# Which engine computes the exact rest of every weight group: VectorE for all of them, where GpSimd had most

## The chip, the cores and the metric

The kernel runs on one core of one Trainium2 chip. The metric is the device time of one execution in microseconds (us). Each core has TensorE (PE in the profile; its weight loads are PEld), VectorE (DVE), ScalarE (ACT), GpSimd (POOL) and SyncE (SP, which here only issues loads). An engine works through its own instructions in the order in which they were issued and waits on semaphores for the others.

## The reference: what is computed

One layer of a decoder with two groups of heads, for a prompt of 512 tokens with 16 meta tokens ahead of it, and for 8 decode sequences of one new token with 2048 cached positions each. Everything is float32.

```
z = rmsnorm(h, norm_g) @ w_in                    # (528 + 8 tokens, 2048) @ (2048, 8192)
hq, hf, hi, hg, aq, ak, av, ag = split(z)        # 8 heads of 128 columns each
o_hg = hgrn2(hq, hf, hi, state)                  # recurrent state 128x128 per head
p  = softmax(q k / 8 + bias[distance])           # two softmaxes per head: keys of 64, values of 128
o_at = (p[0] - lam * p[1]) @ v                   # prompt: 528 keys; decode: 2048 cached keys in pages + 1
h  = h + concat(norm(o_hg) * silu(hg), norm(o_at) * silu(ag)) @ w_out
y  = rmsnorm(h, final_norm_g)
```

The new keys and values, the recurrent states and `y` are the outputs. A page holds 128 cached positions of one sequence (512 KB of keys, 512 KB of values); 8 sequences have 16 pages each, so 128 key pages and 128 value pages are read.

## The kernel before, in words

**The dense product.** The columns of `w_in` make 64 blocks of 128 output features (in the order aq0-7, ak0-7, av0-7, then hf, hi, hq per head, then hg0-7, ag0-7), those of `w_out` 16 more. A block has four *groups* of four contraction chunks. TensorE reaches float32 accuracy in three products of the short type float32r: inputs and weights are each cut into a rounded part and the exact rest (xh and xl, hi and lo), and `group` issues hi·xh, hi·xl and lo·xh, 24 products in all. `split(u)` makes the two parts of group u's weights: ScalarE copies the raw weights into `hi`, rounding them, and then `lo = raw - hi` is one TENSOR_TENSOR of 128x512 on VectorE or GpSimd. Line 291 to 292, `lo_on_dve`, says on which. Both parts have four buffers; the split runs LEAD = 3 groups ahead of the product, so the write of `lo` for group u+3 waits until the product of group u-1 has been read.

**The order of issue.** The loop over u (line 1172) issues in each *slot*: `split(u + 3)`, `group(u)`, one stage of every chain that can go on (`step_threads`: prompt attention, HGRN, norms, the softmax of a decode sequence), and then `fill()`. At the end each engine is tied to the order in which its instructions were issued (line 1223).

**Decode attention on VectorE.** A key page is one multiplication of 128x1024 with the broadcast query (`pgt<-pgt,qb`) and one reduction (`scd<-pgt`). A value page is eight instructions of 128x128, one per head: `acc += page * weight` (SCALAR_TENSOR_TENSOR; for a sequence's first page TENSOR_SCALAR). `steps` lists the 256 passes: the keys run three sequences ahead of the values, and the last 48 passes are the values of sequences 5, 6 and 7. `page_step` issues half a pass. After a sequence's values `pv_end` sums `acc` over the partitions with eight products `t_o`; the next sequence's values reuse the one `acc` buffer and so wait for them.

**The planner.** `fill()` issues page passes while `clock["dve"] < clock["pe"] + LATE`. `Clock` and `Counted` keep rough costs for every instruction issued, per engine; they decide only the order. An instruction counted on VectorE takes the place of page passes in that slot.

**The loop at the end of the input blocks.** In the last slots of `w_in` (block 63 = ag7, from its second group on, line 1181) everything that the gated outputs need must have been issued: a `while` loop calls `step_threads()` and `page_step()` until the norms of both halves are in (`hnorm`, `dnorm`). Only then come groups 1 to 3 of block 63, the split of the gated outputs (mh, ml) and the 16 blocks of `w_out`. Any page passes still left at that point are issued inside this loop, between two groups of TensorE.

Of the kernel before, what the change touches and what calls it, by code (L numbers as in the profile page):

```python
# [20 lines left out]
KC = D // P            # contraction chunks  # L21
SEQ = 512
NS = 8                 # decode sequences
NM = 16                # meta tokens
# columns: meta tokens, prompt, decode; the blocks whose meta tokens reach no output leave those out
CK = NM + SEQ + NS
CQ = SEQ + NS
S0 = SEQ               # first decode column without meta columns
K0 = NM + SEQ          # and with them
# [8 lines left out]
W = 656                # period of the bias row: a strip's 528 columns and 127 rows  # L38
# [9 lines left out]
def shape_constants():  # L48
    """Matrices that depend on the shapes alone."""
    ident = np.eye(P, dtype=np.float32)  # L50
    t = np.arange(P)
    pair = ((t[:, None] // CHUNK == t[None, :] // CHUNK) & (t[:, None] <= t[None, :])).astype(np.float32)
    scan = np.ones((P, CK), np.float32)
    scan[:, 0] = 0.0
    scan[:, NM:K0:CHUNK] = 0.0
    scan[:, K0:] = 0.0
    cst = np.concatenate([ident, pair, scan], axis=1)
    # one-hot rows of buckets (row 32: masked) for: the prompt's bias row, decode's far, near and new keys
    x = np.arange(W)
    dist = 400 - np.where(x < 528, x, x - W)  # L60
    strip = np.where(dist >= 0, rel_bucket(dist), 32)
    far = np.full(P, rel_bucket(np.array(129)))
    near = rel_bucket(P - np.arange(P))
    new = np.zeros(P, np.int64)
    cols = np.concatenate([strip, far, near, new])
    oh = (np.arange(33)[:, None] == cols[None, :]).astype(np.float32)
    return cst, oh
# [6 lines left out]
class Clock:  # L74
    """Rough times at which the engines finish what has been issued, for the order of issue."""
# [11 lines left out]
    def tile(self, t, tag, bufs):  # L87
        """A tile in a ring of buffers: its first writer waits for the readers of the buffer's last tile."""
        ring = self.rings.setdefault(tag, [])
        name = t.tensor.name  # L90
        if len(ring) == bufs:
            old = ring.pop(0)
            self.read[name] = max(self.read.get(old, (0.0, ""))[0], self.written.get(old, (0.0, ""))[0]), ""
        ring.append(name)
        return t
# [15 lines left out]
    def arrive(self, ap, mb):  # L111
        """A load that is issued now."""
        start = max(self.now["dma"], self.now["pe"], self.now["dve"])
        self.now["dma"] = start + mb * 3.0
        self.written[ap.tensor.name] = self.now["dma"] + 2.0, "dma"


class Counted:
    """An engine whose instructions' rough times are kept."""
# [33 lines left out]
def layer_kernel(ctx: ExitStack, tc: tile.TileContext, A):  # L153
# [20 lines left out]
    def expln():  # L174
        """The table with both the exponential and the logarithm."""
        if table[0] != EXPLN:
            nc.scalar.preload_act_table_set(EXPLN)
            table[0] = EXPLN
            clock.now["act"] += 1.3
# [49 lines left out]
    def keep_warm(n):  # L229
        """Products that nobody reads, for TensorE's clock."""  # L230
        for _ in range(n):
            T.matmul(warm[:, :P], ones, ones, start=True, stop=True)

# [1 line left out]
    GK = 4  # L235
    NPB = 6                     # pages on chip
    NG = KC // GK
    LEAD = 3                    # groups by which the split of the weights runs ahead
# [5 lines left out]
    blocks = []                 # (name, weights, halves of columns)  # L244
# [17 lines left out]
    LASTP = ((0, 256), (256, CQ))       # the last block in parts, so that little is left to store at the end  # L262
# [5 lines left out]
    def load_raw(i):  # L268
        """Half of a block's weights."""
        b, z = divmod(i, 2)  # L270
        if b < NB:
            raws[i] = wp.tile([P, KC // 2, P], F32, name="raw", tag="raw", bufs=3)
            clock.arrive(raws[i], 0.5)
            (store if i > 2 else load)(out=raws[i], in_=blocks[b][1][z * D // 2:(z + 1) * D // 2, :].rearrange("(k p) n -> p k n", p=P))

    def split(u):
        """High part of a group of weights, rounded to float32r, and the exact rest."""
# [13 lines left out]
    def lo_on_dve(b, g):  # L291
        return b == 1 or (0 < b < 8 and g % 2 == 0) or (b >= NIN and g == 1)
# [55 lines left out]
    # the norm's weights to every partition; to columns for the meta and decode tokens  # L348
# [34 lines left out]
    # the first block's first half runs while the rest of the prompt is transposed  # L383
# [46 lines left out]
    # the small parameters  # L430
# [19 lines left out]
    dp = hw.tile([P, 2, 64], F32, name="dp", tag="dp")  # L450
    dlv = dl.rearrange("p (a b c) -> p a b c", a=2, b=2)
    nlam = cp.tile([P, 1], F32, name="nlam")      # minus lambda
# [12 lines left out]
    def small_constants():  # L465
# [15 lines left out]
        # the prompt's bias by distance, negated: a row per head, skewed through DRAM into a strip per head  # L481
# [31 lines left out]
    aq = mp.tile([P, H, CQ], F32, name="aq")            # -q/8, then the attention half of mixed  # L513
    ak = [None] * H
    hgm = [None] * H                                      # the HGRN half of mixed
# [9 lines left out]
    ktail = [cp.tile([P, 2 * NM], F32, name=f"kt{i}") for i in range(2)]     # the last keys of a head, its two parts apart  # L525
# [4 lines left out]
    # Each group of the dense product is followed by one stage of every chain that can go on; decode  # L530
    # attention's passes over pages fill VectorE up to the time that TensorE has reached.
# [27 lines left out]
    def fill():  # L559
        """Passes over pages until VectorE's work reaches to TensorE's present time."""  # L560
# [8 lines left out]
    def later(slots, **k):  # L569
        """A store some slots from now, so that its queue's engine needn't wait."""  # L570
        def gen():
            yield slots
            store(**k)
        spawn(gen())

# [7 lines left out]
    KA = 3                      # sequences by which the keys run ahead of the values  # L583
# [29 lines left out]
    def page_step():  # L613
        """Half of a page's pass."""
# [115 lines left out]
    def to_tok(src, h, name, tag, dst, dst_s):  # L730
        """Rows 0..511 in four blocks, the last 16 and decode's in a fifth."""
# [18 lines left out]
    def norm_chain(o, n, g, name, sq=None):  # L750
        """o *= g / sqrt(mean over partitions of o^2 + eps)"""
# [33 lines left out]
    def attn():  # L785
        live = {}
        for n in range(4 * H + 4):
# [6 lines left out]
            if i4:                      # output of the block  # L794
# [10 lines left out]
            if i3:                      # transposed weights  # L805
# [11 lines left out]
            if i1:                      # exponentials  # L817
# [4 lines left out]
            if n < 4 * H:               # scores  # L822
# [12 lines left out]
            if i2:                      # difference of the two softmaxes  # L835
# [10 lines left out]
            if n < 4 * H:               # maximum  # L846
# [193 lines left out]
    def mix_split(k, c0, c1):  # L1040
        """Columns of the gated outputs in two exact parts, in place of the inputs'."""
# [8 lines left out]
    def decode_norm(k0):  # L1050
        """The decode columns of a half of mixed, gated."""
# [8 lines left out]
    def decode_mix(gg):  # L1060
        """The decode columns of four heads of mixed, in two exact parts."""
# [12 lines left out]
    def out_load(q):  # L1074
        """A quarter of the residual's columns."""
# [11 lines left out]
    def squares(q, j0, j1, s):  # L1087
        """Sums of squares; ScalarE and VectorE take turns."""
        for j in range(j0, j1):
            square(xr[q][:, j, :], P, stat[0][:, j, q:q + 1], j % 2)  # L1090
        if s:
            square(xsm[q], NS, stat[0][:NS, 4, q:q + 1], True)
# [33 lines left out]
    def out_last(z, ps):  # L1126
        """A half of the last block and the norm of its tokens."""
# [129 lines left out]
```

## Time and profile before

| | |
|---|---|
| runs (us) | 1349.47, 1352.16, 1352.70: median 1352.16 |
| the profiled execution, first to last instruction | 1346.6 us |
| TensorE busy, share of the span | 1218.8 us, 91% |
| weight loads | 1150.8 us, 85% |
| VectorE busy | 946.8 us, 70% |
| GpSimd busy | 590.0 us, 44% |
| ScalarE busy | 545.0 us, 40% |
| mean granted TensorE clock | 0.951 |

The runs lie 2.9 to 6.1 us above the profiled span; the median lies 5.6 us above it. A share of the span is an average over stages: the start, key pages beside the attention projections, prompt attention, HGRN, the gate blocks, and the output projection.

### The profile page before, as it was taken

The numbers are of one execution on the slowest core, as the hardware profiler recorded it, in microseconds if no ns is written. First come the engines' busy times: TensorE is split into PE (matmuls) and PEld (weight loads), VectorE is DVE, ScalarE is ACT, GpSimd is POOL, SyncE is SP. The second block draws the span as 40 slices with busy tenths as digits, with TensorE's granted clock in tenths as the row PEclk, the third lists the DMA queues.
The fourth block names the chain that finished last, engine by engine and source line by source line (L and its number), as shares of the span: only waits on it lengthen the run. The fifth ranks groups of instructions, "written<-read, shape, count | busy, mean of one in ns | idle before, by whom it ended". The sixth has DMA issues, their size and how long they took to land. (4 is left out here: it accounts for less than half of the span.)

```text
span 1346.6 us, 25420 instructions
## 1 busy us (share of the span) xinstructions
PE 1218.8 (91%) x9260; PEld 1150.8 (85%) x9260; DVE 946.8 (70%) x1945; ACT 545.0 (40%) x1286; POOL 590.0 (44%) x415
## 2 busy tenths in 40 slices
PE   8999999999999999889979897989973849999995
PEld 6999999887787999789979897889973849999995
DVE  7410899977787879989999999999996544222123
ACT  6322232365566635445535443434310115232233
POOL 3123455422222434345343442534789684344350
PEclk9999999999999999899998998979986969999998
DMA  6453899844544567677786768769676532732323
GB/s 214 121 137 99 304 351 308 281 154 143 150 144 141 187 190 236 217 247 227 233 261 223 241 211 259 237 208 297 205 244 202 179 111 87 232 92 79 95 79 128
DMA packets 240961, 261.05 MB, mean 194 GB/s; under 512 B 8783, under 2 KB 198962, under 8 KB 240171
## 3 DMA queue, kind: packets, MB, share of 16 engines
q1 hardware_dynamic: 57298, 164.09, 36.3%
q10 hardware_dynamic: 183538, 95.34, 25.0%
q8 instruction: 73, 1.20, 0.4%
q14 instruction: 52, 0.43, 0.1%
HBM read 245.94 MB, written 16.14 MB: 195 GB/s over the span
## 5 line engine op out<-in xcount | busy, mean ns | idle before, releaser
L128 POOL TENSOR_TENSOR lo<-raw,hi 128x512 fp32r<-128x512 f32 x288 | 477.3, 1663 | 693.3 <-ACT hi L128 546.6
L128 PE MATMUL ps<-xh,hi 128*128 128x264 f32 (+2 forms) x2048 | 555.3, 300 | 9.1 <-ACT hv L128 5.7
L128 PE MATMUL ps<-xl,hi 128*128 128x264 f32 (+2 forms) x2048 | 535.6, 290 | 1.1 <-DVE xl L128 1.1
L128 PEld LDWEIGHTS ps<-xh,hi 128*128 128x128 f32 x2048 | 398.5, 195 | 26.3 <-issue 9.9
L128 PEld LDWEIGHTS ps<-xl,hi 128*128 128x128 f32 x2048 | 398.6, 195 | 5.2 <-issue 3.8
L128 PE MATMUL ps<-xh,lo 128*128 128x264 f32 (+2 forms) x2048 | 341.6, 290 | 43.5 <-POOL lo L128 43.5
L128 DVE SCALAR_TENSOR_TENSOR acc<-pgt,wd,acc 128x128 f32<-128x128 f32 x960 | 365.9, 452 | 0.0
L128 PEld LDWEIGHTS ps<-xh,lo 128*128 128x128 f32 x2048 | 292.8, 194 | 43.9 <-POOL lo L128 43.9
L128 ACT CAST hi<-raw 128x512 fp32r<-128x512 f32 x321 | 195.4, 616 | 291.2 <-PE ps L128 180.3
L128 DVE TENSOR_TENSOR pgt<-pgt,qb 128x1024 f32<-128x1024 f32 x128 | 172.4, 1347 | 38.4 <-DMA pgt<-in_cache_k 29.8
L128 DVE TENSOR_REDUCE scd<-pgt 128x16 f32<-128x1024 f32 x128 | 155.4, 1214 | 2.3
L128 PE MATMUL ps<-mh,hi 128*128 128x256 f32 (+1 forms) x512 | 130.0, 286 | 3.0 <-ACT gate L128 1.5
L128 PE MATMUL ps<-ml,hi 128*128 128x256 f32 (+1 forms) x512 | 128.5, 283 | 0.0
L128 PEld LDWEIGHTS ps<-mh,hi 128*128 128x128 f32 x512 | 96.4, 188 | 3.9 <-ACT gate L128 1.7
L128 PEld LDWEIGHTS ps<-ml,hi 128*128 128x128 f32 x512 | 96.5, 188 | 0.0
L128 DVE TENSOR_TENSOR lo<-raw,hi 128x512 fp32r<-128x512 f32 x33 | 34.8, 1059 | 79.7 <-ACT hi L128 79.3
L128 DVE TENSOR_TENSOR xr<-xr,t_y 128x512 f32<-128x512 f32 (+1 forms) x17 | 11.2, 656 | 112.3 <-PE t_y L128 112.3
L128 PE MATMUL ps<-mh,lo 128*128 128x256 f32 (+1 forms) x512 | 82.4, 283 | 0.0
L128 PEld LDWEIGHTS ps<-mh,lo 128*128 128x128 f32 x512 | 70.3, 188 | 0.0
L128 DVE SCALAR_TENSOR_TENSOR p<-p,r,p 128x144 f32<-128x144 f32 (+3 forms) x32 | 18.1, 566 | 41.6 <-ACT p L128 41.5
L128 ACT COPY hgm<-ho 128x128 f32<-128x128 f32 x32 | 8.5, 265 | 86.0 <-PE ho L128 86.0
L128 DVE TENSOR_SCALAR acc<-pgt,wd 128x128 f32<-128x128 f32 x64 | 21.4, 402 | 29.2 <-PE t_o L128 29.2
(227 smaller groups left out, 1214.0 us busy)
## 6 DMA issues: line engine op xcount, KB each, us to landing
pgt<-in_cache_k SPq DMA_DIRECT2D x128, 512.0 KB
pgt<-in_cache_v SPq DMA_DIRECT2D x128, 512.0 KB
raw<-in_w_in ACTq DMA_DIRECT2D x125, 512.0 KB
raw<-in_w_out ACTq DMA_DIRECT2D x32, 512.0 KB
x<-in_x_prompt SPq DMA_DIRECT2D x4, 1024.0 KB
qb<-qd SPq DMA_DIRECT2D x8, 512.0 KB
sd<-in_state_hgrn SPq DMA_DIRECT2D x8, 512.0 KB
vb<-hvd SPq DMA_DIRECT2D x8, 512.0 KB
```

The source lines that it names most:

```text
L128: r = f(*a, **k)
```

## The change

`lo_on_dve` returns True for every group. Before, VectorE had block 1, the even groups of blocks 2 to 7 and one group in four of `w_out`; GpSimd had the rest. Comments and docstrings are taken out as well. No number of the planner is touched, but it now counts every `lo` on VectorE.

```
     def lo_on_dve(b, g):
-        return b == 1 or (0 < b < 8 and g % 2 == 0) or (b >= NIN and g == 1)
+        return True
```

In the listings below, `lo` is a rest, `pgt` a page, `scd` the scores of a sequence, `acc` the sum over value pages; `x8` is eight instructions of the same form.

On VectorE, at the first key pages (beside the blocks of the new keys). Before:

```order
L128 TENSOR_TENSOR pgt<-pgt,qb 128x1024
L128 TENSOR_REDUCE scd<-pgt 128x16
L128 TENSOR_TENSOR pgt<-pgt,qb 128x1024
L128 TENSOR_REDUCE scd<-pgt 128x16
L128 TENSOR_TENSOR pgt<-pgt,qb 128x1024
```

The same place in the change:

```order
L128 TENSOR_REDUCE scd<-pgt 128x16
L128 TENSOR_TENSOR pgt<-pgt,qb 128x1024
L128 TENSOR_TENSOR lo<-raw,hi 128x512
L128 TENSOR_REDUCE scd<-pgt 128x16
L128 TENSOR_TENSOR pgt<-pgt,qb 128x1024
L128 TENSOR_TENSOR lo<-raw,hi 128x512
```

One rest now stands in VectorE's row for every slot, and the slot holds one key pass beside it.

On TensorE, around the loop at the end of the input blocks. Before, the last small product of decode attention, `t_rs` (the norm of its output), stands ahead of the first group of block 63 (`xh_109` is the inputs' group 0, `xh_112` group 3):

```order
L128 MATMUL ps<-xh_112,hi 128x264
L128 MATMUL ps<-xl_116,hi 128x264
L128 MATMUL ps<-xh_112,hi 128x264
L128 MATMUL ps<-xh_112,lo 128x264 x4
L128 MATMUL t_rs<-sqs,ones 128x64
L128 MATMUL ps<-xh_109,hi 128x256
L128 MATMUL ps<-xl_113,hi 128x256
```

In the change, between the last product of group 0 of block 63 and the first of its group 1 (`xh_110`):

```order
L128 MATMUL ps<-xh_109,lo 128x264 x4
L128 MATMUL t_mx<-ident,mx 16x128
L128 MATMUL t_mb<-ident,m_14201 128x16
L128 MATMUL t_sum<-rs,ones 128x16
L128 MATMUL t_o<-ones,acc 128x1 x24
L128 MATMUL t_rs<-sqs,ones 128x64
L128 MATMUL ps<-xh_110,hi 128x256
L128 MATMUL ps<-xl_114,hi 128x256
```

The softmax of sequence 7 (`t_mx`, `t_mb`, `t_sum`) and the sums of three sequences' values (24 products `t_o`) stand now between two groups, with no dense product among them.

On VectorE at the same place, in the change (the row begins with the last two rests ahead of the loop and ends with the next rest behind it):

```order
L128 TENSOR_TENSOR lo<-raw,hi 128x512 x2
L128 TENSOR_REDUCE m_14201<-t_mx 16x1
L128 TENSOR_SCALAR acc<-pgt,wd 128x128 x8
L128 SCALAR_TENSOR_TENSOR acc<-pgt,wd,acc 128x128 x12
...
L128 SCALAR_TENSOR_TENSOR acc<-pgt,wd,acc 128x128 x92
L128 TENSOR_SCALAR acc<-pgt,wd 128x128 x8
L128 SCALAR_TENSOR_TENSOR acc<-pgt,wd,acc 128x128 x120
L128 TENSOR_SCALAR acc<-pgt,wd 128x128 x8
L128 SCALAR_TENSOR_TENSOR acc<-pgt,wd,acc 128x128 x120
...
L128 TENSOR_TENSOR lo<-raw,hi 128x512
```

All 48 value passes of sequences 5, 6 and 7 stand behind the products `t_mx` that follow group 0 of block 63. Before, all 256 passes were issued by the first group of block 62.

## Rows read from the trace of the kernel before

**Rows 1.** Stretches of 100 us: length, engines' busy (instructions), granted clock, DMA share, GB/s.

```profile
200.00:300.00 100.00, 97.48 (x726) 88.75 (x725) 88.97 (x153) 41.39 (x112) 43.33 (x39) 0.98 0.78 250
300.00:400.00 100.00, 96.50 (x662) 78.57 (x661) 75.13 (x230) 60.02 (x176) 24.36 (x28) 1.00 0.48 149
400.00:500.00 100.00, 98.28 (x718) 87.53 (x717) 79.20 (x175) 58.63 (x157) 35.28 (x27) 0.98 0.55 170
500.00:600.00 100.00, 89.66 (x673) 85.89 (x672) 91.78 (x161) 46.77 (x112) 42.63 (x31) 0.93 0.76 237
600.00:700.00 100.00, 94.22 (x736) 89.67 (x735) 95.16 (x173) 49.83 (x124) 45.85 (x31) 0.98 0.73 229
700.00:800.00 100.00, 89.44 (x657) 84.88 (x657) 94.92 (x176) 47.29 (x119) 41.57 (x28) 0.91 0.74 239
800.00:900.00 100.00, 85.77 (x625) 80.97 (x623) 92.68 (x177) 40.29 (x104) 41.78 (x30) 0.91 0.72 228
900.00:1000.00 100.00, 90.80 (x679) 89.52 (x680) 93.80 (x231) 31.01 (x55) 65.28 (x39) 0.90 0.80 243
1000.00:1100.00 100.00, 56.48 (x440) 56.07 (x439) 65.80 (x245) 13.71 (x28) 85.92 (x26) 0.78 0.57 180
```

**Rows 2.** TensorE's waits over the span: total, times, longest, in us.

```profile
PE ps L128 <- POOL lo L128: 43.5, 2, 22.4
PE ho L128 <- DVE am L128: 27.9, 13, 7.0
PE t_o L128 <- DVE acc L128: 9.6, 3, 7.5
```

**Rows 3.** VectorE in order of time, 925 to 1145: start, length, instruction.

```profile
944.65 0.28 DVE L128 TENSOR_REDUCE m<-t_mx 16x1 f32<-16x128 f32 x1 [4.00 <-PE t_mx L128]
...
960.62 14.14 DVE L128 SCALAR_TENSOR_TENSOR acc<-pgt,wd,acc 128x128 f32<-128x128 f32 x20
...
977.10 0.16 DVE L128 TENSOR_TENSOR wnew<-scd 128x8 f32<-128x8 f32 x1
...
994.90 3.99 DVE L128 TENSOR_SCALAR acc<-pgt,wd 128x128 f32<-128x128 f32 x8 [1.89 <-PE t_o L128]
998.82 31.59 DVE L128 SCALAR_TENSOR_TENSOR acc<-pgt,wd,acc 128x128 f32<-128x128 f32 x120
1057.71 2.70 DVE L128 TENSOR_SCALAR acc<-pgt,wd 128x128 f32<-128x128 f32 x8 [27.30 <-PE t_o L128]
...
1132.39 0.69 DVE L128 TENSOR_TENSOR lo<-raw,hi 128x512 fp32r<-128x512 f32 x1
1133.00 3.62 DVE L128 TENSOR_TENSOR ml<-hgm,mh 128x512 fp32r<-128x512 f32 x4
```

**Rows 4.** The rests (`lo`) over the span: duration min/median/max in ns, first and last start.

```profile
L128 POOL TENSOR_TENSOR lo<-raw,hi x288: 1256/1292/31678, 14.4 to 1320.2; 128x512 fp32r<-128x512 f32 x144
L128 DVE TENSOR_TENSOR lo<-raw,hi x33: 684/693/4487, 40.1 to 1313.6; 128x512 fp32r<-128x512 f32 x33
```

**Rows 5.** The page's costliest groups, two of them: busy us, mean ns of one, idle before.

```profile
L128 POOL TENSOR_TENSOR lo<-raw,hi 128x512 fp32r<-128x512 f32 x288 | 477.3, 1663 | 693.3 <-ACT hi L128 546.6
...
L128 DVE SCALAR_TENSOR_TENSOR acc<-pgt,wd,acc 128x128 f32<-128x128 f32 x960 | 365.9, 452 | 0.0
```

**Rows 6.** The instructions of the value pages over the span: duration min/median/max in ns.

```profile
L128 DVE SCALAR_TENSOR_TENSOR acc<-pgt,wd,acc x960: 331/343/1523, 294.3 to 1092.6; 128x128 f32<-128x128 f32 x192
```

**Rows 7.** The rests alone by stretch: PE, PEld, DVE, POOL busy (instructions), clock, DMA.

```profile
100.00:1126.00 1026.00, 308.23 (x1840) 264.13 (x1840) 1.54 (x3) 396.53 (x227) 0.94 0.68 214
```

**Rows 8.** Two stretches, all engines: columns as in rows 1.

```profile
998.82:1030.41 31.59, 10.35 (x87) 10.14 (x85) 31.59 (x121) 2.52 (x5) 30.56 (x1) 0.71 0.80 253
1031.59:1035.80 4.21, 4.21 (x19) 4.21 (x20) 0.00 (x0) 1.24 (x2) 4.21 (x5) 0.50 0.40 119
```

**Rows 9.** TensorE in order of time, 1085 to 1140.

```profile
1115.10 1.84 PE L128 MATMUL t_o<-ones,acc 128*128 128x1 f32 x16
...
1122.66 0.33 PE L128 MATMUL t_rs<-sqs,ones 128*128 128x64 f32 x2
```

## The prediction

> **What bounds the kernel now.** I read the stretches of 100 us first [rows 1], because the share of busy time mixes stages. From 200 to 500 TensorE is busy 96 to 98% at a granted clock of 0.98 to 1.00: it is the bound there, although VectorE is busy up to 89%. From 500 to 1000 it falls to 86 to 94% at a clock of 0.90 to 0.98, and VectorE stands at 92 to 95%; from 1000 to 1100 TensorE is down to 56%. Next the waits of TensorE [rows 2]: two of 22.4 and 21.1 us for a rest computed by GpSimd, 43.5 together; 27.9 us in 13 times for `am`, the masked scores of HGRN that VectorE copies; 9.6 us for sums of value pages.
>
> Then why GpSimd's rests and VectorE's copies are late. A rest takes GpSimd 1.29 us at the median, yet the longest took 31.68 us [rows 4]. In that time VectorE ran 120 value-page instructions back to back in 31.59 us, one per 0.263 us [rows 3]: GpSimd "worked" 30.56 of the 31.59 us on one instruction [rows 8]. The reverse is in the same list: at 960.62, beside GpSimd's rests, 20 of these instructions took 14.14 us, 0.707 each. Over the span one lasts 452 ns in the mean [rows 5] and 343 at the median [rows 6], so 960 x 0.109 = 105 us of VectorE's time are waiting inside instructions. The two engines get in each other's way, and TensorE pays at two places: directly when a rest starves, and through VectorE's lateness in the HGRN stage.
>
> The Trainium skill's page "SBUF — State Buffer", section "Who interferes with whom", says that a VectorE instruction with two SBUF inputs and a GpSimd instruction that reads SBUF exclude each other for a whole instruction. The rows above agree with that (31.68 us of starving; 0.707 instead of 0.263 us).
>
> **What the change takes away.** (1) Without rests on GpSimd the waits of 43.5 us have no cause left. What follows them goes too: after the first, TensorE ran 4.21 us at a clock of 0.50 [rows 8]; I count half of it, 2.1 us, and 1.5 us (an estimate by the first) for the second. Together 47.1 us. A rest on VectorE is issued three groups ahead, at the head of its slot, so it is done well before its product; nothing in the value passes can starve it.
>
> (2) The stretch 500 to 1000. TensorE's busy time there is 449.9 us; weighted with the clock of each row (89.66 x 0.93 + 94.22 x 0.98 + 89.44 x 0.91 + 85.77 x 0.91 + 90.80 x 0.90) it is 416.9 us of work at full clock. From 300 to 500 the same product gives 96.50 x 1.00 + 98.28 x 0.98 = 192.8 of 200 us, 0.964. If 500 to 1000 ran like that, it would take 416.9 / 0.964 = 432.5 us: 67.5 us come back. The bounds: nothing, if the waits for `am` come from VectorE's row order and not from its lateness; or 500 - 416.9 = 83 us. I take 67.5 because VectorE's load will be like that of the stretches that run well. Its sum from 200 to 1100 is 777 us [rows 1]. Out go 105 us of waiting and 106 us of passes that move behind this stretch (below); in come the rests. GpSimd did 227 between 100 and 1126 [rows 7], some 205 of them after 200 at an even rate; VectorE needs 0.69 us for one, and its next instruction began 0.61 us after it [rows 3], so 125 to 141 us. That leaves 691 to 707 us of work in about 811 (from 200 to the new start of the loop: `t_rs` at 1122.66 stands ahead of group 0 of block 63 [rows 9], which so ended near 1126, and 1126 - 47.1 - 67.5 = 1011): 85 to 87%, less than the 89% (200 to 300) beside which TensorE was 97.5% busy.
>
> The skill's page "Perfetto Trace Analysis", section "Optimizing Scalar/DVE Operations", speaks against the change: since the two engines share a read port, moving work between them might not help. For VectorE's busy time the rows say the same: 125 to 141 us in, 105 out. By that rule alone the time would stay at 1352; by my sum the rests are not what decides, since GpSimd's own waits and the order of the passes count too.
>
> **What it adds.** (3) The planner counts each rest on VectorE and so fills less into each slot: the row orders show one key pass per slot where two halves followed each other freely, and at the end 48 value passes (sequences 5, 6, 7) are left. They are issued in the loop after group 0 of block 63, when TensorE has only `t_mx`, `t_mb`, `t_sum`, `t_o` and `t_rs` to do. Before, these passes ran under blocks 58 to 62 [rows 3]. Now TensorE stands still for them:
>
> - 360 instructions `acc<-pgt,wd,acc` at 0.263 us (31.59 / 120): 94.8 us; 24 that start a sequence, at 2.70 per eight: 8.1 us.
> - sequence 7's softmax among them: nine small instructions, the first 0.28 us (944.65), the last 0.16 (977.10), together some 2.8 us.
> - two handovers of the one `acc` buffer to `t_o`: VectorE was idle 1.89 us for one when TensorE stood ready [rows 3]: 3.8 us.
> - ahead of it `t_mx` and the reduction of it, some 0.5 us; behind it the last sums: 16 products and loads `t_o` in 1.84 us, `t_rs` 0.33 [rows 9], and three short steps of about 0.3 us between: 3.2 us.
> - TensorE then starts at half clock, as at 1031.59: 2.1 us.
>
> Together 115.3 us. From below 111 (the ends overlapped, no clock loss); from above 137 + 20 = 157, if each of the 360 took the 0.381 us that the span shows (365.9 / 960, [rows 5]), but GpSimd has next to nothing to do beside them. The loads don't set it: 48 pages of 0.524 MB are 25.2 MB, five of them loaded ahead, so 22.5 MB; at the 253 GB/s of the former run of such passes [rows 8] that is 89 us, less than VectorE's 103.
>
> (4) At the start, four rests enter VectorE's row, which TensorE waits for there: 4 x 0.69 = 2.8 us at most, nothing if it no longer waits for GpSimd there; I take 1.5. In `w_out` TensorE is the bound, VectorE is mostly free, and the rests are three groups ahead: nothing. The removed comments do nothing.
>
> **The sum.** 115.3 + 1.5 - 47.1 - 67.5 = +2.2 us on the profiled 1346.6, so 1348.8; with the 5.6 us by which the median lies above it, 1354.4. I predict 1355. The change pays for what it wins: the stalls go, and a hole of about the same length opens between two groups.
>
> **The rivals.**
>
> *Slower: the HGRN stage keeps its stalls.* If the 13 waits for `am` and the lowered clock come from where the passes stand in VectorE's row, the rests lengthen that row and nothing of the 67.5 us comes back: 115.3 + 1.5 - 47.1 = +70, 1422. With half of it, 1388. For it: VectorE stays over 85% busy, and rests now stand between the passes. Against it: 400 to 500 already holds HGRN work with VectorE at 79%, and TensorE was 98% busy there. It decides from the point where less than about 60 us come back.
>
> *Faster: VectorE never makes TensorE wait.* All 83 us come back, and some of the 10 us that 200 to 500 lack in [rows 1]: 115.3 + 1.5 - 47.1 - 83 = -13, 1339, and 1334 with half of those 10 us. For it: the rests bind VectorE to TensorE's groups, so it can't be taken far off by a burst. Against it: no stretch of the trace runs quite without waits, and HGRN has waits for ScalarE too.
>
> *The passes don't run at 0.263 us in the loop* (the loads, or the queue that issues them, hold them up): at 0.33 us, 24 us more, 1379.
>
> **How the numbers follow.** My forecast (1344 to 1366) has 0.42, the slower rival 0.26, the faster one 0.24, the slow loop 0.08. Within 0.3% (1348.1 to 1356.2), about what a measurement can tell from no change, lies over half of the forecast's share: 0.25. Faster by more: 0.24 and the forecast's lower end, 0.30. Slower by more: 0.45. The range of 1336 to 1396 leaves out the end of the slower rival and the tip of the faster one.
>
> **What would show it.** (1) No wait of TensorE for a rest, GpSimd busy about 113 us (590.0 of the table less the 477.3 of [rows 5]). (2) From 500 on a clock of 0.97 or more, TensorE over 95% busy, waits for `am` under 10 us; the mean of `acc<-pgt,wd,acc` near 350 ns. (3) One hole in TensorE's row of about 110 us that begins near 1011 and ends near 1127, with 360 + 24 instructions of VectorE in it; `t_o` and `t_rs` its only products. (4) The first dense product no more than 3 us later. The prediction is wrong if the hole begins well after 1030 (the stalls stayed), before 1000 (TensorE ran better than ever before), or if it is longer than 125 us.

## The result, and the profile after

The change takes 1326.82 us (median of four runs, 1325.25 to 1329.92), where the kernel before took 1350.82 beside it: ratio 0.983, 95% interval 0.981 to 0.985. That is 24 us less, and 28 less than the 1355 forecast; the time lies below the range of 1336 to 1396. The profiled execution spans 1328.1 us and took 1329.92 itself.

The stretches of 100 us of the change, columns as in [rows 1]:

```profile
200.00:300.00 100.00, 99.56 (x752) 90.43 (x752) 87.23 (x160) 43.79 (x116) 3.41 (x13) 1.00 0.71 222
300.00:400.00 100.00, 98.16 (x674) 80.06 (x673) 75.67 (x217) 60.85 (x177) 4.15 (x12) 1.00 0.47 144
400.00:500.00 100.00, 99.61 (x744) 89.15 (x744) 83.14 (x203) 62.01 (x157) 8.42 (x7) 1.00 0.54 166
500.00:600.00 100.00, 97.84 (x763) 94.06 (x762) 84.25 (x171) 51.67 (x130) 14.03 (x8) 0.97 0.70 223
600.00:700.00 100.00, 99.35 (x769) 95.10 (x768) 94.26 (x197) 53.56 (x133) 15.08 (x8) 0.97 0.79 243
700.00:800.00 100.00, 97.62 (x743) 93.14 (x742) 85.70 (x184) 51.59 (x129) 13.51 (x8) 0.96 0.74 230
800.00:900.00 100.00, 99.68 (x812) 97.20 (x811) 94.53 (x199) 43.44 (x97) 33.69 (x16) 0.99 0.84 264
900.00:1000.00 100.00, 100.00 (x832) 99.67 (x830) 95.07 (x204) 30.70 (x56) 23.45 (x18) 1.00 0.80 258
1000.00:1100.00 100.00, 8.22 (x38) 7.77 (x36) 95.97 (x371) 0.76 (x3) 0.00 (x0) 0.51 0.71 221
```

From 200 to 1000 TensorE hardly stops (the number behind the length, 97.6 to 100, at a clock of 0.96 to 1.00); then it stands still for a whole row, in which VectorE is 96% busy. TensorE's waits, as in [rows 2]:

```profile
PE t_o L128 <- DVE acc L128: 88.3, 3, 31.5
PE t_sum L128 <- DVE rs L128: 7.2, 1, 7.2
PE t_x L128 <- DVE x L128: 4.2, 5, 1.7
PE ho L128 <- DVE am L128: 4.0, 3, 2.0
```

The wait for a rest is gone (43.5 before), that for `am` has fallen from 27.9 to 4.0, and TensorE waits 95.5 us (88.3 and 7.2) for VectorE's value pages and softmax, where it waited 9.6 for the sums of value pages before. VectorE in the hole, in order of time (start, length, instruction, idle before):

```profile
1000.17 0.28 DVE L128 TENSOR_REDUCE m<-t_mx 16x1 f32<-16x128 f32 x1 [1.69 <-PE t_mx L128]
1000.38 1.64 DVE L128 TENSOR_SCALAR acc<-pgt,wd 128x128 f32<-128x128 f32 x8
...
1011.63 24.23 DVE L128 SCALAR_TENSOR_TENSOR acc<-pgt,wd,acc 128x128 f32<-128x128 f32 x92
1037.76 1.66 DVE L128 TENSOR_SCALAR acc<-pgt,wd 128x128 f32<-128x128 f32 x8 [1.89 <-PE t_o L128]
1039.33 31.59 DVE L128 SCALAR_TENSOR_TENSOR acc<-pgt,wd,acc 128x128 f32<-128x128 f32 x120
1072.74 1.66 DVE L128 TENSOR_SCALAR acc<-pgt,wd 128x128 f32<-128x128 f32 x8 [1.83 <-PE t_o L128]
1074.32 31.59 DVE L128 SCALAR_TENSOR_TENSOR acc<-pgt,wd,acc 128x128 f32<-128x128 f32 x120
1105.82 0.22 DVE L128 TENSOR_TENSOR wnew<-wnew,avS 128x64 f32<-128x64 f32 x1
```

And TensorE at its two ends, the last products of group 0 of block 63 and the first of group 1:

```profile
999.38 0.65 PE L128 MATMUL ps<-xh,lo 128*128 128x264 f32 x4
999.87 0.27 PE L128 MATMUL t_mx<-ident,mx 128*16 128x128 f32 x1
...
1108.56 0.69 PE L128 MATMUL t_rs<-sqs,ones 128*128 128x64 f32 x2 [0.80 <-ACT sqs L128]
1109.01 0.56 PE L128 MATMUL ps<-xh,hi 128*128 128x256 f32 x1
```

The same products of group 0 in the kernel before:

```profile
1125.29 0.65 PE L128 MATMUL ps<-xh,lo 128*128 128x264 f32 x4
```

The hole lasts 109.0 us, from 1000.0 to 1109.0. Group 0 ended at 1125.9 before, so 125.9 us are won ahead of the hole; behind it 219.1 us follow where 220.7 did. The span's difference is -125.9 + 109.0 - 1.6 = -18.5 us.

### The profile page after: what moved, and what is told of

The parts are those of the page before. It is cut to its first block, busy times and chain, and to the rows that moved or that the text cites. A ratio compares the mean times of both kernels' runs of the same rounds, so it can differ in the third digit from the quotient of the medians.

```text
span 1328.1 us, 25286 instructions
## 1 busy us (share of the span) xinstructions
PE 1200.3 (90%) x9260; PEld 1136.5 (86%) x9260; DVE 1004.0 (76%) x2233; ACT 546.7 (41%) x1286; POOL 143.4 (11%) x127
## 5 line engine op out<-in xcount | busy, mean ns | idle before, releaser
L128 PE MATMUL ps<-xh,hi 128*128 128x264 f32 (+2 forms) x2048 | 546.7, 297 | 2.3 <-ACT ak L128 1.9
L128 PE MATMUL ps<-xl,hi 128*128 128x264 f32 (+2 forms) x2048 | 527.7, 287 | 1.1 <-DVE xl L128 1.1
L128 PEld LDWEIGHTS ps<-xh,hi 128*128 128x128 f32 x2048 | 392.2, 191 | 16.3 <-issue 7.1
L128 PEld LDWEIGHTS ps<-xl,hi 128*128 128x128 f32 x2048 | 391.8, 191 | 5.2 <-issue 5.1
L128 DVE TENSOR_TENSOR lo<-raw,hi 128x512 fp32r<-128x512 f32 x321 | 238.9, 754 | 175.3 <-ACT hi L128 175.1
L128 DVE SCALAR_TENSOR_TENSOR acc<-pgt,wd,acc 128x128 f32<-128x128 f32 x960 | 267.7, 355 | 0.0
L128 DVE TENSOR_TENSOR pgt<-pgt,qb 128x1024 f32<-128x1024 f32 x128 | 156.9, 1226 | 14.2 <-DMA qb<-qd 7.0
L128 PE MATMUL t_o<-ones,acc 128*128 128x1 f32 x128 | 20.1, 287 | 89.0 <-DVE acc L128 88.3
L128 PEld LDWEIGHTS t_o<-ones,acc 128*128 128x128 f32 x128 | 20.0, 245 | 89.5 <-issue 57.0
L128 POOL TENSOR_TENSOR xr<-xr,gfin 128x2048 f32<-128x2048 f32 x3 | 14.3, 4773 | 261.0 <-DMA raw<-in_w_out 176.8
```

Of the source, the lines that this page charges most:

```text
L128: r = f(*a, **k)
```

## The experiments

The change does two things: another engine computes the rests, and, since the planner counts them on VectorE, every row's order differs (48 value passes move into the loop). My theory A: the quiet GpSimd gives the time back (no starving, no waiting inside VectorE's instructions), the order only opens the hole. Theory B: the order itself, with 48 passes fewer on VectorE beside HGRN and the gates, gives most of it. Times are medians, ratios are to the kernel before on the same chip.

**One part at a time.** `e1_old_order`: the rests on VectorE, but counted by the planner as GpSimd's where they were, so that every row has the order of before. (In this kernel and the next, `lo_on_dve` is that of the kernel before again; its line is not shown.)

```
+    VP = Counted(nc.vector, clock, "pool")
-        (V if lo_on_dve(b, g) else G).tensor_tensor(lo, raw, ...)
+        (V if lo_on_dve(b, g) else VP).tensor_tensor(lo, raw, ...)
```

> All rests on VectorE, but the planner books them where it booked them before, so every engine's row is that of the kernel before and no page pass is left for the loop between groups 0 and 1 of block 63. Theory A (the shared port: GpSimd's rests slowed VectorE and were starved by it; the 109 us hole is the price of the planner's booking): the stalls stay away and the hole is gone; VectorE's work from 200 to 1000 is then 691 + 106 = some 800 us of 800, so a few stalls come back: a span of 1225 to 1275 us, TensorE's largest wait under 15 us. Theory B (TensorE was relieved because 48 passes left VectorE's row, not because GpSimd is quiet): VectorE is over-booked, the waits for am are at least the 28 us of before: a span of 1300 to 1360.

Measured: 1303.0 us, ratio 0.965 (0.962 to 0.968), a span of 1298.2 for the profiled execution: faster than both kernels, yet well above what theory A gives and just below theory B's range. The waits for `am` came to 16.0 us, below the 28 that theory B wanted.

`e2_new_order` is the reverse: GpSimd computes as before, the planner counts VectorE.

```
+    GD = Counted(nc.gpsimd, clock, "dve")
-        (V if lo_on_dve(b, g) else G).tensor_tensor(lo, raw, ...)
+        (V if lo_on_dve(b, g) else GD).tensor_tensor(lo, raw, ...)
```

> GpSimd computes the rests that it computed before, but the planner books them on VectorE, so every row is that of the change, with 48 passes in the loop. Theory A: GpSimd and VectorE get in each other's way as before (mean of acc<-pgt,wd,acc at 430 ns or more outside the loop), the HGRN stage loses its 43 us again, the hole of 109 us stays: 1365 to 1410 us. Theory B: the rows decide, so about the time of the change: 1325 to 1340.

Measured: 1359.07 us, ratio 1.004 (1.002 to 1.007): above theory B and below theory A, so neither holds alone. To see where each part acts I take ScalarE's last copy out of gate block 11, a mark that lies ahead of the hole in both orders. Its row in the timeline (start, length, instruction) of the order of before with VectorE, of the new order with GpSimd (both copies in one row), and of the change:

```profile
1031.73 0.39 ACT L128 ACTIVATE gate<-ps 128x264 f32<-128x264 f32 x1 [1.02 <-PE ps L128]
```
```profile
986.32 0.67 ACT L128 ACTIVATE gate<-ps 128x256 f32<-128x256 f32 x2 [4.18 <-DMA pgt<-in_cache_v]
```
```profile
960.72 0.39 ACT L128 ACTIVATE gate<-ps 128x264 f32<-128x264 f32 x1 [1.02 <-PE ps L128]
```

In the kernel before it ended at 1064.0:

```profile
1063.60 0.39 ACT L128 ACTIVATE gate<-ps 128x264 f32<-128x264 f32 x1 [1.08 <-PE ps L128]
```

So, in us of the profiled executions (end of this copy / from there to the end / span):

| | rests on GpSimd | rests on VectorE |
|---|---|---|
| order of before | 1064.0 / 282.6 / 1346.6 | 1032.1 / 266.1 / 1298.2 |
| order of the change | 987.0 / 372.9 / 1359.9 | 961.1 / 367.0 / 1328.1 |

Down a column is the order, along a row the engine. Up to gate block 11 the order alone wins 77.0 us, the engine alone 31.9; both together 102.9. Each of the two removes the first starving rest (22.4), so their sum counts it twice. Behind the mark the order costs 90 to 101 us. (By the medians the order alone is 7 us slower than the kernel before, 1359.07 against 1351.83, and not the 13 of these spans; the engine alone is 49 faster.) From ScalarE's copy of `hf` of head 1 (the block that opens the second HGRN head) to the end of gate block 7 TensorE waits for no rest in any of the four: it took 472.8 us before, 459.7 with the engine alone, 436.2 with the order alone and 418.7 with both. There the order is worth 37 to 41 us and the engine 13 to 18, so theory A gives the smaller part. By stretches of time it is the same: with the order of before and a quiet GpSimd, TensorE was busy 467 of the 500 us from 500 to 1000, with the order of the change and GpSimd at work 478 (before: 449.88, the sum of [rows 1]).

```profile
500.00:1000.00 500.00, 467.28 (x3547) 448.20 (x3546) 471.83 (x1087) 219.95 (x524) 84.59 (x46) 0.95 0.79 247
```
```profile
500.00:1000.00 500.00, 478.05 (x3698) 461.64 (x3696) 458.51 (x775) 222.30 (x527) 249.88 (x180) 0.96 0.73 231
```

In the order of before VectorE is as full as ever (471.83, where it was 468.34): the rests put back what the waiting had cost. The prediction weighed the Trainium skill's page "Perfetto Trace Analysis", section "Optimizing Scalar/DVE Operations", by which moving work between these two engines might not help. This trace agrees for VectorE's busy time. The kernel's time fell by 48 us all the same, and most of that lies behind gate block 7, where the two rests had starved: from there to the end of group 0 of block 63 it took 147.4 us before and 101.9 with the engine alone. The order of the change has no wait for a rest even with GpSimd: its longest rest there takes 2.9 us, and the long runs of value pages fall in the hole, where GpSimd does nothing.

**The port by itself.** `e3_dup`: the change, and GpSimd repeats its former rests in place in the raw weights; nothing reads them.

```
+        if not (b == 1 or (0 < b < 8 and g % 2 == 0) or (b >= NIN and g == 1)):
+            nc.gpsimd.tensor_tensor(raw, raw, hi.bitcast(F32), op=ALU.subtract)
```

> The change, and GpSimd computes each of its former rests once more, in place in the raw weights, when VectorE is done with them; nobody reads that result. The output is that of the change. Theory A: the instructions of GpSimd alone bring VectorE's waiting back: mean of acc<-pgt,wd,acc over 420 ns, TensorE's waits between 500 and 1000 over 25 us, 1350 us or more. Theory B: nothing waits for these instructions but the next load of raw weights, so within 5 us of the change: 1322 to 1335.

Measured: 1399.94 us, ratio 1.036 (1.033 to 1.040), 73 us over the change, as theory A had it (its mean of 420 ns is just missed). From its page, the engines and the two groups:

```profile
PE 1215.9 (87%) x9260; PEld 1148.1 (82%) x9260; DVE 1108.6 (79%) x2233; ACT 543.7 (39%) x1286; POOL 533.7 (38%) x415
...
L288 POOL TENSOR_TENSOR raw<-raw,hi 128x512 f32<-128x512 f32 x288 | 412.9, 1438 | 831.9 <-DVE lo L128 417.5
...
L128 DVE SCALAR_TENSOR_TENSOR acc<-pgt,wd,acc 128x128 f32<-128x128 f32 x960 | 328.8, 416 | 0.0
```

The same 2233 instructions keep VectorE busy for 1108.6 us instead of 1004.0: 105 us of waiting inside instructions. The Trainium skill's page "SBUF — State Buffer", section "Who interferes with whom", says that a VectorE instruction with two SBUF inputs contends with a GpSimd instruction that reads SBUF; this trace agrees (416 ns for a multiply-add instead of 355). The size of 73 us is not the port's alone, though. The added instruction is now the last reader of a buffer of raw weights, so the buffer comes free later, and ScalarE, which issues the next load into it, stands in its own row until then: 179.9 us in 45 waits. TensorE also waits 14.5 us for HGRN work of GpSimd (`kd` and `qe`) that stands behind the added instructions, and for none in the change.

**VectorE's load by itself.** If the port acts through VectorE's time, any work on VectorE should do the same. `e10_heavy`: VectorE computes the rests of blocks 24 to 61 twice, uncounted by the planner, so that the order stays.

```
+        if 24 <= b < 62:
+            nc.vector.tensor_tensor(raw, raw, hi.bitcast(F32), op=ALU.subtract)
```

> The change, with 152 more instructions on VectorE: in blocks 24 to 61 (HGRN and gates) it computes every rest a second time, in place in the raw weights, uncounted by the planner, so that the passes stand as in the change; some 95 to 100 us more of VectorE's time. Theory (load for each slot): VectorE had 45 us free from 500 to 1000, so TensorE now waits for it, 50 to 75 us in all, and the hole of 109 us stays: 1380 to 1400 us; the wait for am and for ACT gate come back. Rival (order): TensorE runs as in the change, 1327 us, at most 15 us more.

Measured: 1412.5 us, ratio 1.047 (1.043 to 1.051), 86 us over the change and 12 above the range that the theory gave; the rival falls. VectorE's busy time rose by 116.5 us (1004.0 to 1120.5), so 0.74 us of each came through; in `e3_dup` it was 73 of 105, 0.70. The waits of before are back:

```profile
PE ps L128 <- ACT gate L128: 21.4, 10, 4.8
PE ho L128 <- DVE am L128: 20.2, 12, 6.0
```

Here too the added instruction holds the raw weights, and ScalarE waits for it 98.4 us in 28 times. Those that end at a gate's copy, in `e3_dup` and here (us in total, times, longest):

```profile
ACT gate L128 <- POOL raw L288: 42.0, 8, 6.7
ACT gate L128 <- DVE raw L288: 30.6, 6, 5.9
```

So the two prices of 0.70 and 0.74 agree, but both hold this path and are no price of VectorE's load alone. The path itself is in the real kernels as well, and it is one way in which a late VectorE reached TensorE in the gate blocks: the rest comes late, the load of weights behind it in ScalarE's row (ACTq) is held, and so is the gate's copy that TensorE waits for. In `e1_old_order`, where TensorE waited 18.8 us for gates, a rest ends at 1004.60, the load is issued at 1004.64, and the gate's copy follows after 9.32 us of idle ScalarE:

```profile
1003.93 0.67 DVE L128 TENSOR_TENSOR lo<-raw,hi 128x512 fp32r<-128x512 f32 x1
1004.64 0.37 ACTq L275 DMA_DIRECT2D raw<-in_w_in  x1
1005.11 0.67 ACT L128 ACTIVATE gate<-ps 128x256 f32<-128x256 f32 x2 [9.32 <-DVE acc L128]
```

No kernel was run in which another engine issues these loads.

`e9_light` goes the other way, from the kernel of the next part in which no pass is left for the loop: four of eight heads are left out of the value pages of sequences 1 to 6 beyond the first page, counted by the planner all the same.

```
+                if g > 0 and 0 < s < 7 and h % 2:
+                    clock.issue("dve", 0.065 + P / 960 + 0.06, [acc], [vt, w, acc])
+                    continue
```

> The kernel with the planner's costs of TensorE times 1.2 (no pass left in the loop, every row's order as there), with the multiply-adds of four of the eight heads left out in all but the first page of sequences 1 to 6, but counted by the planner as before: 360 instructions fewer, some 130 us of VectorE's time between 490 and 1035. Theory (the waits of the HGRN and gate blocks come from how much VectorE has to do for each slot of TensorE): the last gate block ahead of block 63 is reached as in the change or sooner, 65 to 75 us earlier, and nothing is left to pay: about 1225 to 1235 us. Rival (they come from where single passes stand in VectorE's row): about 1299 us as there, at most 15 us less.

Measured: 1263.6 us (1248.92 to 1264.34), ratio 0.932 (0.926 to 0.939): 35 us less than the 1298.65 with all heads, for 92.5 us less of VectorE's time. From 500 to 1000 TensorE is nearly as busy as in the change (494.5, the sum of its column above):

```profile
500.00:1000.00 500.00, 488.39 (x3805) 472.54 (x3804) 411.59 (x824) 229.99 (x541) 71.74 (x52) 0.96 0.81 264
```

So load counts there, but the size was off by half, 35 us instead of 65 to 75. The copy of gate block 14, the last ahead of block 63, ended at 1036.5, 40.7 us later than in the change (995.8). Of these, 15 were lost by the first HGRN block, which was reached at 440, as without the cut: this planner packs the key stage (200 to 300: TensorE 93.13, VectorE 95.56 busy) ahead of the cut, a loss of order. The other 25 came behind it, and no run tells whether by order or by load.

**How many passes to leave.** The planner's rough costs of TensorE set how many passes it fits in. `e4_pe120`, `e5_pe110` and `e6_pe115` multiply them:

```
+            if self.name == 'pe':
+                t *= 1.2        # 1.10 in e5_pe110, 1.15 in e6_pe115
```

> The change, and the planner counts TensorE's costs 1.2 times as high, so that fill() puts more page passes into each slot; all 256 are issued before the loop, none in it. Theory A: no hole, VectorE busy 93 to 97% from 200 to 1000 without waiting for GpSimd, TensorE short of 30 us of waits: 1225 to 1265 us. Theory B: VectorE's row is as full as before the change, so the waits for am and the lowered clock of 500 to 1000 come back: 1290 to 1330.

> The change with the planner's costs of TensorE times 1.10: 25 value passes are left for the loop after group 0 of block 63, where the change leaves 48 and the factor 1.2 none. Theory (the passes cost about the same wherever VectorE does them; in the loop each costs 2.1 us of standing TensorE and gives back 1.4 us before it, so a net of 30 us / 48 = 0.62 us for each one left): hole of about 25 x 2.1 + 8 = 60 us, time 1299 + 25 x 0.62 = 1314 us. Rival (the relief of the HGRN and gate blocks saturates: a few passes out of their row remove all the waits, some 79 us): 1299 + 60 - 79 = 1280 us.

> The same with a factor of 1.15: 17 passes are left. Theory: hole of about 17 x 2.1 + 8 = 44 us, time 1299 + 17 x 0.62 = 1309 us. Rival (saturation): 1299 + 44 - 79 = 1264 us.

| passes left | group 0 of block 63 ends | next dense product | hole | median | ratio (95%) |
|---|---|---|---|---|---|
| 0 (`e4_pe120`) | 1075.5 | 1078.2 | 2.7 | 1298.65 | 0.961 (0.958 to 0.964) |
| 17 (`e6_pe115`) | 1029.3 | 1076.4 | 47.1 | 1298.36 | 0.961 (0.959 to 0.964) |
| 25 (`e5_pe110`) | 1021.7 | 1083.5 | 61.8 | 1304.88 | 0.966 (0.963 to 0.969) |
| 48 (the change) | 1000.0 | 1109.0 | 109.0 | 1326.82 | 0.983 (0.981 to 0.985) |

From the next dense product to the end it is 219.1 to 219.9 us in all four, so the third column decides. `e4_pe120` lies in theory B's range, and theory A falls. A pass in the loop costs 1.8 to 2.6 us each time. What it gives back can't be read from the second column alone, because the factor 1.2 also packs the key stage: `hf` of head 0 ended at 441.1 in `e4_pe120`, at 422.9, 424.6 and 425.7 in the others, so 18 of the 46 us between the first two rows were lost before HGRN began. From that copy to the end of group 0 it took 634.4, 606.4, 597.1 and 574.3 us: a pass gave back 1.6 us for each of the first 17 (28.0 / 17), then 1.2 (9.3 / 8), then 1.0 (22.8 / 23), less than it cost each time. The times forecast for `e5_pe110` and `e6_pe115` were about 10 us too slow, since they were counted from the 1299 of `e4_pe120`, which held that loss; the rival, full saturation, is wrong too. By the medians the first 17 cost nothing, and the other 31 of the change cost 28 us. The waits of TensorE in `e6_pe115` show the passes in the loop (first line) and what is left of the waits ahead of it:

```profile
PE t_o L128 <- DVE acc L128: 40.5, 4, 31.5
PE ho L128 <- DVE am L128: 9.7, 8, 3.8
PE ps L128 <- ACT gate L128: 9.3, 7, 2.0
```

**The hole by itself.** Two kernels with the change's rows up to the hole. `e8_none` leaves out sequences 5 to 7 beyond their first page, loads and all; `e7_quarter` keeps the loads and two of eight heads.

```
+                if g > 0 and s > 4:              # e8_none; its loads are skipped too
+                    continue
+                if g > 0 and s > 4 and h % 4:    # e7_quarter
+                    continue
```

> The change, with the instructions of six of the eight heads left out for all but the first page of sequences 5, 6 and 7 (the loads stay): in the loop 90 instead of 360 multiply-adds, every row before it as in the change. Theory (VectorE sets the hole): it loses 270 x 0.263 = 71 us, so 38 us remain, unless the loads of 43 pages, 89 us at 253 GB/s, now bind: then it shrinks only to about 80 to 90 us, and the time goes to about 1300 to 1308 us; without the loads 1256. Rival (the loads bound the hole already): no change, 1327 us.

> The change, with these pages' loads and instructions left out altogether (sequences 5, 6 and 7 keep their first page): every row before the loop stays as in the change, the loop has 24 multiplications, the softmax of sequence 7 and the products t_o. Theory (the hole is the 360 multiply-adds and nothing else, and nothing later depends on its length): 95 us less, a hole of 14 us, 1232 us. Rival (other work waits in the loop too, such as the norm of the HGRN output or the weights' loads, which the passes cover): a hole of 30 us or more, 1248 us or more.

Measured: `e8_none` 1229.29 us, ratio 0.911 (0.908 to 0.914), a hole of 14.6 us: as the theory had it, within 3 us. `e7_quarter` 1284.66 us, ratio 0.951 (0.947 to 0.954), a hole of 70.9 us; neither the 38 without the loads' limit nor the 80 to 90 with it. The loads do bind there, but faster than forecast: VectorE in the loop waits for each page,

```profile
1006.74 0.61 DVE L128 SCALAR_TENSOR_TENSOR acc<-pgt,wd,acc 128x128 f32<-128x128 f32 x2 [0.94 <-DMA pgt<-in_cache_v]
1007.99 0.61 DVE L128 SCALAR_TENSOR_TENSOR acc<-pgt,wd,acc 128x128 f32<-128x128 f32 x2 [0.63 <-DMA pgt<-in_cache_v]
1009.27 0.61 DVE L128 SCALAR_TENSOR_TENSOR acc<-pgt,wd,acc 128x128 f32<-128x128 f32 x2 [0.67 <-DMA pgt<-in_cache_v]
```

a page (one line above) every 1.25 to 1.28 us there, and 365 GB/s over a longer stretch:

```profile
1005.00:1060.00 55.00, 7.11 (x32) 6.97 (x32) 25.00 (x91) 0.33 (x2) 0.00 (x0) 0.50 0.94 365
```

The 253 GB/s of [rows 8] was VectorE's demand, not what the loads can do. These two also show how well one profiled execution can be read: with the rows of the change, they reached the end of group 0 at 995.4 and 991.8, where the change did at 1000.0.

**Better versions.** `e11_late125` uses 1.10 until prompt attention is issued and 1.25 after, to spare the key stage and leave no pass; `e12_gates125` 1.15, and 1.25 in the gate blocks (12 passes left).

```
+                t *= self.clock.factor
+        clock.factor = (1.1, 1.1, 1.25, 1.25)[ph]      # e12_gates125: (1.15, 1.15, 1.15, 1.25)
```

> The change, with the planner's costs of TensorE times 1.10 until prompt attention is issued and times 1.25 from then on; no pass is left in the loop. The kernel with 1.2 throughout had lost 15 us to the change by the first HGRN block, beside the key pages, and won them back only at the end. Theory (with VectorE's load as the limit, work that is taken off the key stage waits for VectorE later): hf of head 0 near 425 us as in the change, HGRN and gates some 15 us slower than with 1.2, 1295 to 1300 us. Rival (the key stage's loss is a loss by itself): about 1285 us.

> The change, with a factor of 1.15 and 1.25 in the gate blocks alone; 12 passes are left, where 1.15 throughout left 17. Theory (the first passes left in the loop give back about what they cost): no different from 1.15 throughout, 1295 to 1300 us. Rival (each one left costs a net of 0.62 us, from the change against the factor 1.2): 3 us less than with 1.15, at most.

Measured: `e11_late125` 1289.54 us, ratio 0.956 (0.953 to 0.958), the fastest of the kernels that compute everything, 59 below the 1348.82 of the kernel before beside it and 37 below the change. It reached the first HGRN block at 425 instead of 441, and kept 7 (by the ratios) to 9 (by the medians) of those 16 us: between the theory and the rival. VectorE is fuller than anywhere, 483.34 us of 500:

```profile
500.00:1000.00 500.00, 462.28 (x3570) 443.00 (x3570) 483.34 (x1115) 220.22 (x525) 84.01 (x48) 0.97 0.79 252
```

`e12_gates125` 1294.87 us, ratio 0.960 (0.957 to 0.962), which both theories allow within the noise. With the key stage alike, the count of passes left now stands by itself: `hf` of head 0 ended at 424.9 (none left), 425.0 (12) and 422.9 (17, `e6_pe115`), and from there to the first dense product behind the loop it took 644.3, 650.9 and 653.5 us. So even the first passes left in the loop don't pay for themselves; that `e4_pe120` and `e6_pe115` take the same time comes from the key stage.

## Why the prediction was wrong

The mechanism was forecast as it came, and its large terms were nearly right; what failed is the remainder of two terms of 113 and 115 us, where all the small errors fell on one side.

- **(1) Starving.** Right: TensorE has no wait for a rest left. (GpSimd's busy time, 143.4 us on the page, lies above the 113 forecast; nothing waits for it.) But `e2_new_order` shows that the order alone removes it as well. The two gate blocks that held the starving took 36.2 and 35.2 us before and 11.6 each in the change: 48.2, where I counted 47.1.
- **(2) The stretch 500 to 1000.** The size was right. The same product of busy time and clock is 97.84 x 0.97 + 99.35 x 0.97 + 97.62 x 0.96 + 99.68 x 0.99 + 100 x 1.00 = 483.7 of 500 us, 0.967, where I took 0.964. VectorE's busy time from 200 to 1000 is 699.8 us (the sum of its column above), where the forecast had 691 to 707. The mean of `acc<-pgt,wd,acc` is 355 ns, as said. The rival that nothing comes back falls. The reason was right in its sum, less so in its stress: the rests put on VectorE (125 to 141) undo the 105 of waiting, and the 106 us of passes that leave the stretch are most of the relief. `e1_old_order` took the first without the second, and TensorE was busy 467 us of 500; `e2_new_order` took the second without the first, 478; both together 494.
- **(4) The stretches before 500: the step that failed.** I counted +1.5 us at the start and nothing more. From 200 to 500 the product of [rows 1] is 288.3 of 300 us, and 297.3 after: 9.0 us came back there, where the prediction had "some of the 10 us that 200 to 500 lack" only in its faster rival. With (2) as forecast that makes the end of group 0 10.5 us earlier; it came 12.8 earlier than the forecast 1012.8 (1011 and the 1.5). ScalarE's copy of `hf` of head 1, near 500, shows the same without the clock. Its row in the kernel before, the change, the engine alone (`e1_old_order`) and the order alone (`e2_new_order`):

```profile
505.27 0.39 ACT L128 ACTIVATE hf<-ps 128x264 f32<-128x264 f32 x1
496.39 0.38 ACT L128 ACTIVATE hf<-ps 128x264 f32<-128x264 f32 x1
514.53 0.39 ACT L128 ACTIVATE hf<-ps 128x264 f32<-128x264 f32 x1
497.43 0.39 ACT L128 ACTIVATE hf<-ps 128x264 f32<-128x264 f32 x1
```

It came 8.9 us earlier where I had it 1.5 later: 10.4 of the 27.6 us that the forecast is off, its largest part. The order did that: alone it gives 7.8 us, the engine alone costs 9.3. I counted what the planner's new booking leaves for the end, and not what it takes off VectorE beside the key pages: from 130 to 430 VectorE was busy 245.4 us before, 260.5 with the engine alone, 212.3 with the order alone and 238.0 in the change, and TensorE 290.8, 286.9, 294.5 and 295.4. From this copy to the end of group 0 it took 117.0 us less (620.2 to 503.2), against the 114.6 of (1) and (2). These are single profiled executions; `e7_quarter` and `e8_none`, with the same rows, end group 0 another 4.6 and 8.2 us earlier. The hole thus began at 1000.0, on the very bound that the prediction gave as a sign of being wrong.
- **(3) The hole.** 109.0 us measured against 113.2 without the clock's term. The multiply-adds took 0.263 us as forecast (31.59 / 120), the handovers 1.89 and 1.83. The instructions that open a sequence took 1.66 us for eight instead of the 2.70 taken from [rows 3], where GpSimd was at work beside them: 3.1 us less for the three.
- **Behind the hole** I added 2.1 us for the half clock; in all, the part behind it became 1.6 us shorter. Nothing here tells why.
- **The median over the span.** I added 5.6 us. The change's own profiled execution took 1.8 us more than its span (1329.92 against 1328.1), and in every run for which both are on record it is 1.7 to 2.0; its median lies 1.3 below that span. So 3.8 of the 5.6 were the luck of a fast profiled execution of the kernel before, and the change's was 3.1 us above its median: 6.9 us together, luck and no mechanism.

Together 12.8 + 4.2 + 3.7 + 6.9 = 27.6 us, which is 1354.4 less 1326.8. The faster rival, "VectorE never makes TensorE wait" with a chance of 0.24, lies nearer to the profile; its 1334 lacked the shorter hole and kept the same 5.6.

What stays open: how the relief of the HGRN and gate stages splits between VectorE's load and the places of single passes. `e10_heavy` and `e3_dup` cost 0.70 to 0.74 us for each us of VectorE's time, ScalarE's held loads included; `e9_light` gave back only 0.38.

## What to carry to other kernels

Where an engine's work is moved in a kernel whose order comes from a planner, the new order can weigh more than the move: here the engine alone was worth -49 us and the order alone +7, and booking the work where it was would have given 1303 us instead of 1327. Work that is pushed to a place without cover costs its full time there, and here it gave back less where it left, down to the last pass. A sweep of a planner's costs moves more than the count that it is meant to move, so compare the marks of an early stage too before its rows are read as a price. An engine that both computes and issues loads passes another engine's lateness on. And when a forecast is the remainder of two large terms, count the small ones of every stretch, and don't add the offset of a single execution.

## What was not expected of the hardware

A GpSimd instruction was kept out for as long as VectorE ran without a gap: 31.68 us for one that takes 1.29 at the median, beside 120 instructions [rows 3, 4]. With the same rests beside VectorE in short runs the longest was 2.9 us. The page loads reached 365 GB/s when VectorE asked for little (`e7_quarter`), where 264 was the most in any 100 us of the change's table above.
